# S5 readout from turned-back states, remainders of every third gate chunk by an adding DMA, and a Tanh behind the Sines

## The chip, the cores and the metric

The kernel runs on one core of one Trainium2 chip. The metric is the device time of one execution in microseconds; the time before is the median of three runs. PE is TensorE (PEld its weight load), DVE is VectorE, ACT is ScalarE, POOL is GpSimd, SP is SyncE. Two of these, SP and POOL, issue the kernel's DMAs.

## What is computed

Two layers of an encoder block on x of 256 frames by 1024 channels, in float32:

```
x += 1/2 * SwiGLU_FFN1(rmsnorm(x))
h = rmsnorm(x)
[u_s5 | q | k | v | z_conv | gate_logits] = h @ w_in
y_s5   = glu(gelu(S5(u_s5))) @ w_br_s5
y_attn = chunked_attention(q, k, v) @ w_br_attn
y_conv = conv_module(z_conv)            (ends in @ w_br_conv)
x += (sum over branches of sigmoid(gate_logits_i + b_i) * y_i) @ w_out
x += 1/2 * SwiGLU_FFN2(rmsnorm(x))
```

The S5 part is a complex diagonal recurrence over time, state[t] = a * state[t-1] + b u[t], in 16 groups of 64 states, and its output is the real part of c times the state plus d u.

## The kernel before

**Weights.** All weights are cut into 128x128 tiles, in the order in which PE reads them (`plan`), and eight tiles make a chunk of 128x1024 (512 KB). There are 382 chunks. For each chunk `fetch` (L391 to L407) loads `raw` on SP's queue (three slots), ACT rounds it to `hi` in the format fp32r (L403), and DVE subtracts to get the remainder `lo` (L404, L405); `hi` and `lo` have four slots each, so that the work on a chunk waits until PE has read the chunk four before it. PE makes each product from the pieces (`prod`, L419 to L439): `hi` with the rounded activations, `hi` with their remainder, and `lo` with the rounded activations. In the feed-forward parts the first two are one product of 512 columns; in the gates all three have 256 columns, and in q, k and v 512.

**Stages.** Per layer: up and down projection of FFN1, the mixer, FFN2. The mixer (L752) multiplies by w_in for the S5 input, the convolution's input (z), q, k and v, then by the 24 column blocks of the gates (23 in a row, one later), the branch projections and w_out. Attention, convolution and S5 run beside the gates' products.

**S5.** The recurrence is done in a rotating frame. `s5_tables` (L637) computes during FFN1's up projection tables of cosines and sines by frame, eight blocks j of 128 states, in `tab` (tile name `tbl`): `angle` prepares them, `sines` (L709) applies the Sine on ACT in two instructions of 128x2048, and `coefs` builds the readout matrices `cc`. In the mixer `s5_states(j)` (L775) copies the input rows to `us` (ACT copies for the first four blocks, 12 DMAs on POOL's queue for the last four), multiplies them by `bs` on PE into the one buffer `pq`, rotates the result with `sa` and `sc` on DVE, scans it over time, and multiplies the scanned values by cosines (into `mc`) and by sines (into `tab`). Every four blocks a readout on PE follows: for each of four column groups four products into `y`, with real part, negated imaginary part, negated real part and negated imaginary part of `cc`, two from `mc` and two from `tab`:

```
for n, (w, i) in enumerate(((0, 0), (2, 1), (1, 1), (2, 0))):
    for q in range(4):
        jj = 4 * b + q
        rhs = (mcs[jj][:, i * T:(i + 1) * T] if n < 2 else st["tab"][:, jj, i, :])
```

ACT's functions come from tables that an instruction ACT_TABLE_LOAD brings in: Sine is in one, Tanh and the exponential in another, and plain copies are in each. The compiler puts a load ahead of an instruction whose function is not in the table at hand.

**Order.** Every instruction is first recorded with the tiles that it reads and writes (`Recorder`), then a planner (`schedule`, L251, and `one_pass`, L288) puts them into one order per engine, by costs (`price`, L222) and due times counted back from PE's queue. The engines then run these orders, each waiting where data is not there. So a change of a cost or an instruction shifts the order elsewhere too. All instructions are issued from one line, L339 (L341 in the change), so that line tells nothing in the profile; the tiles do.

Of the kernel before, what the change touches and what calls it, by code (L numbers as in the profile page):

```python
# [17 lines left out]
F32 = mybir.dt.float32  # L18
F32R = mybir.dt.float32r
I32 = mybir.dt.int32  # L20
AF = mybir.ActivationFunctionType
ALU = mybir.AluOpType
# [3 lines left out]
L, P, T, DM, DFF = 2, 128, 256, 1024, 2816  # L26
# [4 lines left out]
U0, Q0, K0, V0, Z0, G0 = 0, 2, 6, 10, 14, 18  # L31
CHT = 8
# [48 lines left out]
PLAN = plan()  # L81
INDEX = {t: i for i, t in enumerate(PLAN)}
NCH = -(-len(PLAN) // CHT)


PCOLS = {}
# [41 lines left out]
class Recorder:  # L128
# [92 lines left out]
    @staticmethod  # L221
    def price(eng, name, outs, ins, kw):  # L222
        n = 1
        for d in list(outs[0].ap)[1:]:
            n *= d[1]
        if name == "dma_start":
            return (max(0.45, 1.5e-3 * n), 1.8) if eng == "sp" else (1.0, 2.0 + 2.5e-3 * n)
        if eng == "pe":
            if name == "transpose":
                return 0.1, 0.2  # L230
            if n == 1:
                return 0.224, 0.2
            if kw["rhs"].dtype != F32R or n < 256:
                rows = outs[0].partition_size()
                return max(n / 2370.0 * 4 * rows / P, 0.03), 0.2
            return n / 2240.0 + 0.006, 0.2
        scal = 0.06 if any(a.free_size() == 1 for a in ins) and n > 1 else 0
        psum = any(a.space == PSUM for a in outs + ins)
        if eng == "act":
            return 0.12 + n / 1200.0 + scal + (0.1 if kw.get("accum_out") is not None else 0), 0.2  # L240
        if name == "reciprocal":
            return 0.06 + 8 * n / 960.0, 0.16
        if name == "tensor_reduce":
            n = 1
            for d in list(ins[0].ap)[1:]:
                n *= d[1]
        fast = name in ("tensor_scalar", "tensor_copy") and not psum
        rate = 1920.0 if fast else 480.0 if name == "tensor_tensor_scan" else 960.0
        return 0.068 + scal + n / rate + (0.06 if kw.get("accum_out") is not None else 0), 0.16
# [103 lines left out]
class Builder:  # L353
# [37 lines left out]
    def fetch(self, upto):  # L391
        nc = self.nc
        while self.fetched <= min(upto, NCH - 1):
            c = self.fetched
            n = min(CHT, len(PLAN) - c * CHT) * P
            raw = self.tile(self.chunk, [P, CHT * P], F32, "raw", RAW)
            hi = self.tile(self.chunk, [P, CHT * P], F32R, "hi", 4)
            lo = self.tile(self.chunk, [P, CHT * P], F32R, "lo", 4)
            for a, b in PARTS.get(c, [(0, n)]):
                if (c, a) in X_LOADS:  # L400
                    self.load_x(*X_LOADS[c, a])
                nc.sync.dma_start(out=raw[:, a:b], in_=self.w_d[c, :, a:b])
                nc.scalar.copy(out=hi[:, a:b], in_=raw[:, a:b])  # L403
                nc.vector.tensor_tensor(out=lo[:, a:b], in0=raw[:, a:b], in1=hi[:, a:b].bitcast(F32),  # L404
                                        op=ALU.subtract)  # L405
            self.chunks[c] = (hi, lo)
            self.chunks.pop(c - 12, None)  # L407
            self.fetched += 1
# [228 lines left out]
    def s5_tables(self, l):  # L637

        nc = self.nc
# [69 lines left out]
        def sines():  # L709
            for h in range(2):  # L710
                t = st["tab"][:, 4 * h:4 * h + 4, :, :].rearrange("p j r s -> p (j r s)")
                nc.scalar.activation(out=t, in_=t, func=AF.Sin, scale=6.283185)

        steps.append(sines)

        def coefs():
            lr, li, mag = st["lr"], self.par(l, "lim"), st["mag"]
            ar, ai, den, cr, ci, t = (self.small(8, s) for s in ("ar", "ai", "den", "cr", "ci", "ct"))
            tt(out=ar, in0=st["cos"][:, :, 1:2].rearrange("p j o -> p (j o)"), in1=mag, op=ALU.mult)
            ts(out=ar, in0=ar, scalar1=1.0, scalar2=None, op0=ALU.subtract)  # L720
            tt(out=ai, in0=st["sin"][:, :, 1:2].rearrange("p j o -> p (j o)"), in1=mag, op=ALU.mult)
            tt(out=den, in0=lr, in1=lr, op=ALU.mult)
            tt(out=t, in0=li, in1=li, op=ALU.mult)
            tt(out=den, in0=den, in1=t, op=ALU.add)
            nc.vector.reciprocal(out=den, in_=den)
            tt(out=cr, in0=ar, in1=lr, op=ALU.mult)
            tt(out=t, in0=ai, in1=li, op=ALU.mult)
            tt(out=cr, in0=cr, in1=t, op=ALU.add)
            tt(out=cr, in0=cr, in1=den, op=ALU.mult)
            tt(out=ci, in0=ai, in1=lr, op=ALU.mult)  # L730
            tt(out=t, in0=ar, in1=li, op=ALU.mult)
            tt(out=ci, in0=ci, in1=t, op=ALU.subtract)
            tt(out=ci, in0=ci, in1=den, op=ALU.mult)

            c4 = st["ct"].rearrange("p (j r c) -> p j r c", j=8, r=2)
            cc = self.tile(self.res, [P, 8, 3, 32], F32, "cc")
            t2 = self.tmp("sa", 2 * T)[:, :T].rearrange("p (j c) -> p j c", j=8)
            b = lambda v: v.unsqueeze(2).broadcast_to([P, 8, 32])
            tt(out=cc[:, :, 0, :], in0=c4[:, :, 0, :], in1=b(cr), op=ALU.mult)
            tt(out=t2, in0=c4[:, :, 1, :], in1=b(ci), op=ALU.mult)  # L740
            tt(out=cc[:, :, 0, :], in0=cc[:, :, 0, :], in1=t2, op=ALU.subtract)
            ts(out=cc[:, :, 1, :], in0=cc[:, :, 0, :], scalar1=-1.0, scalar2=None, op0=ALU.mult)
            tt(out=cc[:, :, 2, :], in0=c4[:, :, 0, :], in1=b(ci), op=ALU.mult)
            tt(out=t2, in0=c4[:, :, 1, :], in1=b(cr), op=ALU.mult)
            stt(out=cc[:, :, 2, :], in0=cc[:, :, 2, :], scalar=-1.0, in1=t2, op0=ALU.mult, op1=ALU.subtract)
            st["cc"] = cc

        steps.append(coefs)
# [3 lines left out]
    def mixer(self, l, after):  # L752
        nc = self.nc
# [21 lines left out]
        def s5_states(j):  # L775
# [30 lines left out]
            mc = self.tmp("mc", 2 * T)  # L806
            tt(out=v3(mc), in0=v3(z), in1=b3(cosj), op=ALU.mult)
            tt(out=tab, in0=v3(z), in1=b3(sinj), op=ALU.mult)
            mcs.append(mc)
            if j % 4 == 3:  # L810
                b = j // 4
                if b == 0:
                    y_ps[0] = self.bank("y")
                cc = st["cc"]
                nc.together()
                for n, (w, i) in enumerate(((0, 0), (2, 1), (1, 1), (2, 0))):
                    for q in range(4):
                        jj = 4 * b + q
                        rhs = (mcs[jj][:, i * T:(i + 1) * T] if n < 2 else st["tab"][:, jj, i, :])
                        nc.tensor.matmul(y_ps[0][32 * q:32 * q + 32, b * T:(b + 1) * T], lhsT=cc[:, jj, w, :], rhs=rhs,  # L820
                                         start=n == 0, stop=n == 3, tile_position=(0, 32 * q))
                nc.apart()

        mcs = []
# [393 lines left out]
```

## Time and profile before

| | |
|---|---|
| runs | 1139.96 us median of 3 (1139.72 to 1142.24) |
| profiled execution, its own time | 1140.64 us |
| its span | 1138.8 us |
| PE busy | 1130.4 us (99%) |
| DVE busy | 993.3 us (87%) |
| ACT busy | 707.1 us (62%) |
| POOL busy | 13.0 us (1%) |
| share of the 16 DMA engines' time that SP's queue took | 56.3% |

The span is the time from the first to the last instruction. An engine's busy time is the union of its instructions' durations; matmuls overlap, so that their durations are longer than their distance. Idle time of an engine is put down to what ended it ("<-"). The chain of waits goes back from the last instruction, at each step to what released it.

### The profile page before, as it was taken

What the parts mean: (1) busy time and instruction counts of PE and PEld (TensorE: products, weight loads), DVE (VectorE), ACT (ScalarE), POOL (GpSimd) and SP (SyncE); (2) the same over time, 40 slices, a digit from 0 to 9 for tenths busy, and PEclk for the clock granted to TensorE, in tenths of its full rate; (3) what the DMA queues carried; (4) which work ended last, traced back from release to release, by engine and by line L of the source; (5) the groups of instructions that cost most, each with busy time, mean ns of one, the idle gap of its engine ahead of it and who ended that gap; (6) DMA issues with size and microseconds to landing.
All of it is one profiled execution on the core that took longest, in us unless ns stands there. A gap on an engine that the chain in (4) does not pass through costs nothing.

```text
span 1138.8 us, 19885 instructions
## 1 busy us (share of the span) xinstructions
PE 1130.4 (99%) x7246; PEld 1006.7 (88%) x7246; DVE 993.3 (87%) x2089; ACT 707.1 (62%) x1366; POOL 13.0 (1%) x32
## 2 busy tenths in 40 slices
PE   9999999999999999999999999999999999999998
PEld 6888888889999988888888888898899999888887
DVE  7999987999989988886789998879999898888754
ACT  6665765797674665555556657557877556655542
POOL 0000000010000000000000000002000000000000
PEclk9999999999999999999999999999999999999999
DMA  8655567555444665555565555666543556555662
GB/s 258 210 185 186 185 198 236 186 173 168 147 149 157 194 200 186 189 186 186 186 220 185 186 186 171 216 222 189 168 159 130 167 160 199 196 186 185 186 203 93
DMA packets 60322, 209.85 MB, mean 184 GB/s; under 512 B 6976, under 2 KB 9664, under 8 KB 59968
## 3 DMA queue, kind: packets, MB, share of 16 engines
q1 hardware_dynamic: 59072, 207.79, 56.3%
q8 instruction: 57, 0.93, 0.3%
q0 software_dynamic: 1152, 0.79, 0.3%
q14 instruction: 41, 0.34, 0.1%
HBM read 206.72 MB, written 1.05 MB: 182 GB/s over the span
## 4 chain that ended last, share of the span: by engine, by line
PE 96%; ACT 2%; issue 1%; DVE 1%; DMA 0%; SPq 0%; ACTq 0%; DVEq 0%
PE mm L339 65%; PE at L339 17%; PE y L339 7%; PE pq L339 6%; PE ax L339 1%; ACT hi L339 1%; ACT us L339 0%; DMA px<-in_x 0%; SPq L339 0%; DVE sa L339 0%; ACT L339 0%; DVE sc L339 0%; DVE lo L339 0%; ACT gh L339 0%; ACT x L339 0%
## 5 line engine op out<-in xcount | busy, mean ns | idle before, releaser
L339 ACT CAST hi<-raw 128x1024 fp32r<-128x1024 f32 (+1 forms) x385 | 400.5, 1042 | 291.5 <-PE mm L339 121.5
L339 DVE TENSOR_TENSOR lo<-raw,hi 128x1024 fp32r<-128x1024 f32 (+1 forms) x385 | 466.2, 1213 | 111.2 <-ACT hi L339 109.2
L339 PE MATMUL mm<-x,hi 128*128 128x256 f32 (+1 forms) x1600 | 406.3, 331 | 1.3 <-ACT hi L339 1.3
L339 PE MATMUL mm<-x,lo 128*128 128x256 f32 x1120 | 302.8, 282 | 0.1
L339 PEld LDWEIGHTS mm<-x,hi 128*128 128x128 f32 x1600 | 267.8, 188 | 26.5 <-ACT hi L339 2.7
L339 PE MATMUL mm<-AB,hi 128*128 128x512 f32 (+1 forms) x726 | 246.2, 390 | 0.0
L339 PEld LDWEIGHTS mm<-x,lo 128*128 128x128 f32 x1120 | 210.4, 188 | 9.8 <-issue 1.8
L339 PE MATMUL mm<-AB,lo 128*128 128x256 f32 x704 | 193.2, 281 | 0.0
L339 PEld LDWEIGHTS mm<-AB,hi 128*128 128x128 f32 x726 | 133.3, 188 | 28.4
L339 PEld LDWEIGHTS mm<-AB,lo 128*128 128x128 f32 x704 | 133.0, 189 | 2.6
L339 PE MATMUL at<-x,hi 128*128 128x512 f32 x384 | 135.3, 394 | 0.0
L339 PE MATMUL at<-x,lo 128*128 128x256 f32 x384 | 99.8, 279 | 0.0
L339 PEld LDWEIGHTS at<-x,hi 128*128 128x128 f32 x384 | 70.4, 187 | 13.1 <-issue 0.2
L339 PEld LDWEIGHTS at<-x,lo 128*128 128x128 f32 x384 | 72.0, 188 | 4.3
L339 PE MATMUL pq<-x,hi 128*128 128x512 f32 x192 | 69.4, 394 | 0.0
L339 PE MATMUL y<-x,hi 128*128 128x512 f32 x192 | 69.4, 394 | 0.0
L339 ACT CAST AB<-ev 128x256 fp32r<-128x256 f32 x88 | 35.8, 407 | 25.7 <-DVE ev L339 25.5
L339 DVE TENSOR_TENSOR ev<-mm,ev 128x256 f32<-128x256 f32 x111 | 45.5, 417 | 5.6 <-ACT ev L339 5.6
L339 PE MATMUL pq<-x,lo 128*128 128x256 f32 x192 | 49.8, 279 | 0.0
L339 PE MATMUL y<-x,lo 128*128 128x256 f32 x192 | 49.8, 279 | 0.0
L339 ACT COPY ev<-mm 128x256 f32<-128x256 f32 x111 | 39.9, 367 | 14.3 <-PE mm L339 13.0
L339 ACT ACTIVATE th<-ev 128x256 f32<-128x256 f32 x88 | 36.4, 418 | 19.0 <-DVE ev L339 18.7
(264 smaller groups left out, 1598.6 us busy)
## 6 DMA issues: line engine op xcount, KB each, us to landing
raw<-in_w SPq DMA_DIRECT2D x380, 512.0 KB, 4.2
AB<-in_b SPq DMA_DIRECT2D x2, 1536.0 KB, 7.5
mc<-in_s SPq DMA_DIRECT2D x8, 192.0 KB, 5.4
out_x<-px SPq DMA_DIRECT2D x8, 128.0 KB, 3.3
raw<-in_w SPq DMA_DIRECT2D x3, 256.0 KB, 4.6
px<-in_x SPq DMA_DIRECT2D x2, 256.0 KB, 6.0
ct<-in_p SPq DMA_DIRECT2D x2, 256.0 KB, 6.0
us<-gh POOLq DMA_DIRECT2D x16, 32.0 KB, 3.1
```

What stands on the lines that cost most here:

```text
L339: fn(*args, **kw)
```

## The change

Four edits. `s5_states` adds a subtraction and an addition of 128x256 on DVE per block that turn the scanned states back out of the rotating frame, into `mc`; the readout then takes two products per column group, both from `mc`, and `cc` loses the negated real part. For the chunks in `BY_DMA`, every third one that begins in the gates' columns (8 per layer), DVE's subtraction goes: ACT writes minus the rounded weights into `lo`, and a DMA on POOL's queue adds the weights to it, read from HBM again. A Tanh of one column follows the two Sines. The planner's cost of POOL's DMAs becomes 0.6 us and 7.0 us to the landing, whatever the size.

```diff
--- before.py
+++ after.py
@@ -81,6 +81,8 @@
 PLAN = plan()
 INDEX = {t: i for i, t in enumerate(PLAN)}
 NCH = -(-len(PLAN) // CHT)
+
+BY_DMA = [c for c in range(NCH) if PLAN[c * CHT][1] == "w_in" and PLAN[c * CHT][3] >= G0][::3]
 
 
 PCOLS = {}
@@ -224,7 +226,7 @@
         for d in list(outs[0].ap)[1:]:
             n *= d[1]
         if name == "dma_start":
-            return (max(0.45, 1.5e-3 * n), 1.8) if eng == "sp" else (1.0, 2.0 + 2.5e-3 * n)
+            return (max(0.45, 1.5e-3 * n), 1.8) if eng == "sp" else (0.6, 7.0)
         if eng == "pe":
             if name == "transpose":
                 return 0.1, 0.2
@@ -401,6 +403,11 @@
                     self.load_x(*X_LOADS[c, a])
                 nc.sync.dma_start(out=raw[:, a:b], in_=self.w_d[c, :, a:b])
                 nc.scalar.copy(out=hi[:, a:b], in_=raw[:, a:b])
+                if c in BY_DMA:
+
+                    nc.scalar.activation(out=lo, in_=raw, func=AF.Copy, scale=-1.0)
+                    nc.gpsimd.dma_start(out=lo, in_=self.w_d[c].bitcast(F32R), accum_op=ALU.add)
+                    continue
                 nc.vector.tensor_tensor(out=lo[:, a:b], in0=raw[:, a:b], in1=hi[:, a:b].bitcast(F32),
                                         op=ALU.subtract)
             self.chunks[c] = (hi, lo)
@@ -711,6 +718,8 @@
                 t = st["tab"][:, 4 * h:4 * h + 4, :, :].rearrange("p j r s -> p (j r s)")
                 nc.scalar.activation(out=t, in_=t, func=AF.Sin, scale=6.283185)
 
+            nc.scalar.activation(out=self.tanh, in_=st["sin"][:, 7, :1], func=AF.Tanh)
+
         steps.append(sines)
 
         def coefs():
@@ -733,16 +742,15 @@
             tt(out=ci, in0=ci, in1=den, op=ALU.mult)
 
             c4 = st["ct"].rearrange("p (j r c) -> p j r c", j=8, r=2)
-            cc = self.tile(self.res, [P, 8, 3, 32], F32, "cc")
+            cc = self.tile(self.res, [P, 8, 2, 32], F32, "cc")
             t2 = self.tmp("sa", 2 * T)[:, :T].rearrange("p (j c) -> p j c", j=8)
             b = lambda v: v.unsqueeze(2).broadcast_to([P, 8, 32])
             tt(out=cc[:, :, 0, :], in0=c4[:, :, 0, :], in1=b(cr), op=ALU.mult)
             tt(out=t2, in0=c4[:, :, 1, :], in1=b(ci), op=ALU.mult)
             tt(out=cc[:, :, 0, :], in0=cc[:, :, 0, :], in1=t2, op=ALU.subtract)
-            ts(out=cc[:, :, 1, :], in0=cc[:, :, 0, :], scalar1=-1.0, scalar2=None, op0=ALU.mult)
-            tt(out=cc[:, :, 2, :], in0=c4[:, :, 0, :], in1=b(ci), op=ALU.mult)
+            tt(out=cc[:, :, 1, :], in0=c4[:, :, 0, :], in1=b(ci), op=ALU.mult)
             tt(out=t2, in0=c4[:, :, 1, :], in1=b(cr), op=ALU.mult)
-            stt(out=cc[:, :, 2, :], in0=cc[:, :, 2, :], scalar=-1.0, in1=t2, op0=ALU.mult, op1=ALU.subtract)
+            stt(out=cc[:, :, 1, :], in0=cc[:, :, 1, :], scalar=-1.0, in1=t2, op0=ALU.mult, op1=ALU.subtract)
             st["cc"] = cc
 
         steps.append(coefs)
@@ -806,6 +814,8 @@
             mc = self.tmp("mc", 2 * T)
             tt(out=v3(mc), in0=v3(z), in1=b3(cosj), op=ALU.mult)
             tt(out=tab, in0=v3(z), in1=b3(sinj), op=ALU.mult)
+            tt(out=mc[:, :T], in0=mc[:, :T], in1=tab[:, 1, :], op=ALU.subtract)
+            tt(out=mc[:, T:], in0=mc[:, T:], in1=tab[:, 0, :], op=ALU.add)
             mcs.append(mc)
             if j % 4 == 3:
                 b = j // 4
@@ -813,12 +823,12 @@
                     y_ps[0] = self.bank("y")
                 cc = st["cc"]
                 nc.together()
-                for n, (w, i) in enumerate(((0, 0), (2, 1), (1, 1), (2, 0))):
+                for r in range(2):
                     for q in range(4):
                         jj = 4 * b + q
-                        rhs = (mcs[jj][:, i * T:(i + 1) * T] if n < 2 else st["tab"][:, jj, i, :])
-                        nc.tensor.matmul(y_ps[0][32 * q:32 * q + 32, b * T:(b + 1) * T], lhsT=cc[:, jj, w, :], rhs=rhs,
-                                         start=n == 0, stop=n == 3, tile_position=(0, 32 * q))
+                        nc.tensor.matmul(y_ps[0][32 * q:32 * q + 32, b * T:(b + 1) * T], lhsT=cc[:, jj, r, :],
+                                         rhs=mcs[jj][:, r * T:(r + 1) * T], start=r == 0, stop=r == 1,
+                                         tile_position=(0, 32 * q))
                 nc.apart()
 
         mcs = []
```

ACT's order at the first Tanh of the second layer's mixer (`th` of the convolution's gate, from `sc`; `us` the copies for S5, `hi` a rounded chunk). Before:

```order
L339 CAST us_1915<-gh_1723 32x256 x4
L339 CAST us_1915<-gl_1724 32x256
L339 CAST hi_1740<-raw_1739 128x1024
L339 ACT_TABLE_LOAD
L339 ACTIVATE th_1734<-sc_1733 128x256
L339 CAST us_1915<-gl_1724 32x256
```

In the change:

```order
L341 CAST us_1915<-gh_1723 32x256 x4
L341 CAST us_1915<-gl_1724 32x256 x2
L341 CAST hi_1740<-raw_1739 128x1024
L341 ACTIVATE th_1734<-sc_1733 128x256
L341 CAST us_1915<-gh_1723 32x256
```

The load of the table has left this place, and one copy into `us` has moved ahead of the cast.

DVE's order in the second layer's mixer up to the last reading of the second pair of S5 input products (`sc_1922`), which frees `pq` for the third pair. Before:

```order
L339 TENSOR_TENSOR lo_1750<-raw_1748,hi_1749 128x1024
L339 TENSOR_TENSOR sa_1921<-pq_1920,tbl_1325 128x512
L339 TENSOR_TENSOR sc_1742<-mm_1735,rb_1715 128x512
L339 TENSOR_TENSOR sa_1917<-sa_1917,sc_1918 128x256 x2
L339 TENSOR_TENSOR lo_1753<-raw_1751,hi_1752 128x1024
L339 SCALAR_TENSOR_TENSOR hp_1725<-th_1743,sc_1742 128x256
L339 SCALAR_TENSOR_TENSOR sa_1917<-mag_1374,sa_1917 128x256
L339 TENSOR_TENSOR sc_1922<-pq_1920,tbl_1325 128x512
```

In the change:

```order
L341 TENSOR_TENSOR lo_1750<-raw_1748,hi_1749 128x1024
L341 TENSOR_TENSOR sa_1921<-pq_1920,tbl_1325 128x512
L341 TENSOR_TENSOR sc_1742<-mm_1735,rb_1715 128x512
L341 TENSOR_TENSOR sa_1917<-sa_1917,sc_1918 128x256 x2
L341 SCALAR_TENSOR_TENSOR sa_1917<-mag_1374,sa_1917 128x256
L341 SCALAR_TENSOR_TENSOR hp_1725<-th_1743,sc_1742 128x256
L341 SCALAR_TENSOR_TENSOR sa_1917<-mag_1374,sa_1917 128x256
L341 TENSOR_TENSOR sc_1922<-pq_1920,tbl_1325 128x512
```

One remainder (`lo_1753`) now stands behind the reading, and the second scan (out of `mag`) ahead of it.

ACT's order at the first gate chunk of the second layer (`lo_1786` and `hi_1785`, from `raw_1784`; `jk` are sums of squares for the attention's norms). In the change:

```order
L341 ACTIVATE jk_1828,ss_1727_1824<-nat_1775 128x64
L341 ACTIVATE lo_1786<-raw_1784 128x1024
L341 CAST hi_1785<-raw_1784 128x1024
L341 CAST x_1520_1617<-ev_1791 128x256
```

and POOL's order around it:

```order
L341 DMA us_1933<-gl_1724 32x256
L341 DMA us_1933<-gh_1723 32x256
L341 DMA lo_1786<-in_w 128x1024
L341 DMA lo_1963<-in_w 128x1024
```

The negated rounded weights are written ahead of the cast, and the adding DMAs stand on POOL's queue behind the copies for S5. Before, `lo_1786` was a subtraction on DVE behind the cast.

## Rows read from the trace of the kernel before

**Rows 1.** The page, parts 1 and 2: PE's busy time; its granted clock in 40 slices.

```profile
PE 1130.4 (99%) x7246; PEld 1006.7 (88%) x7246; DVE 993.3 (87%) x2089; ACT 707.1 (62%) x1366; POOL 13.0 (1%) x32
...
PEclk9999999999999999999999999999999999999999
```

**Rows 2.** Waits of PE: us in total, times, longest us.

```profile
PE pq L339 <- DVE sc L339: 1.8, 2, 0.9
PE mm L339 <- ACT hi L339: 1.3, 2, 1.0
```

**Rows 3.** Both mixers: length, busy PE, PEld, DVE, ACT, POOL; clock, DMA share, GB/s.

```profile
198.00:390.00 192.00, 191.10 (x1485) 177.98 (x1484) 182.63 (x409) 134.62 (x316) 6.00 (x12) 1.00 0.53 171
763.00:950.00 187.00, 186.09 (x1453) 173.34 (x1451) 179.03 (x399) 133.94 (x315) 5.81 (x12) 1.00 0.52 167
```

**Rows 4.** Timeline of PE at the first readout: start us, us, instruction.

```profile
248.24 1.07 PE L339 MATMUL y<-mc,cc 128*32 128x256 f32 x16
249.13 1.05 PE L339 MATMUL y<-tbl,cc 128*32 128x256 f32 x16
250.11 0.50 PE L339 MATMUL at<-hi,x 128*128 128x512 f32 x1
```

**Rows 5.** Instructions on tile cc: count, shortest/median/longest ns, first and last start.

```profile
L339 PE MATMUL y<-tbl,cc x64: 379/379/379, 249.1 to 855.3; 128*32 128x256 f32 x64
...
L339 DVE TENSOR_SCALAR cc<-cc x2: 294/294/294, 159.3 to 713.1; 128x256 f32<-128x256 f32 x2
```

**Rows 6.** Groups by form, whole span: count, busy us, mean ns, idle before.

```profile
L339 DVE TENSOR_TENSOR lo<-raw,hi 128x1024 fp32r<-128x1024 f32 x380 | 463.3, 1221 | 109.9 <-ACT hi L339 108.1
L339 ACT CAST hi<-raw 128x1024 fp32r<-128x1024 f32 x380 | 397.8, 1049 | 290.5 <-PE mm L339 121.5 <-issue 65.3 <-PE at L339 42.4
...
L339 DVE TENSOR_TENSOR sa<-sa,sc 128x256 f32<-128x256 f32 x32 | 12.6, 414 | 0.0
```

**Rows 7.** Chain of waits at the second layer's third pair: start us, us, what.

```profile
771.52 1.28 ACT L339
...
781.10 0.68 DVE sc L339
...
781.92 0.47 PE pq L339 x2
782.39 2.79 PE at L339 x12
```

**Rows 8.** Timeline of DVE ahead of that pair, its idle time in brackets.

```profile
773.26 0.43 DVE L339 SCALAR_TENSOR_TENSOR hp<-th,sc 128x256 f32<-128x256 f32 x1 [0.50 <-ACT th L339]
...
776.02 1.23 DVE L339 TENSOR_TENSOR lo<-raw,hi 128x1024 fp32r<-128x1024 f32 x1 [1.14 <-ACT hi L339]
...
779.03 1.22 DVE L339 TENSOR_TENSOR lo<-raw,hi 128x1024 fp32r<-128x1024 f32 x1
780.17 0.42 DVE L339 SCALAR_TENSOR_TENSOR hp<-th,sc 128x256 f32<-128x256 f32 x1
```

**Rows 9.** Timeline of PE there, with products of 256 columns ahead of it.

```profile
772.17 0.28 PE L339 MATMUL mm<-x,lo 128*128 128x256 f32 x1
...
772.53 0.28 PE L339 MATMUL mm<-x,lo 128*128 128x256 f32 x1
...
780.61 0.40 PE L339 MATMUL at<-hi,x 128*128 128x512 f32 x1
781.92 0.36 PE L339 MATMUL pq<-us,bs 96*128 96x256 f32 x1 [0.91 <-DVE sc L339]
```

**Rows 10.** Tile us: POOL's issues of its copies (ns), and their landings.

```profile
L339 POOL DMA_DIRECT2D us<-gh x16: 492/497/632, 225.7 to 794.9; - x16
...
DMA to landing us min/median/max: 2.2/3.2/4.3
```

**Rows 11.** Tile raw, 198 to 350 us: landings of the loads of 512 KB.

```profile
DMA to landing us min/median/max: 3.5/3.7/4.8
```

**Rows 12.** Groups by form on DVE, 198 to 350 us: its longest TENSOR_SCALAR.

```profile
L339 DVE TENSOR_SCALAR cv<-hp,px,db 128x256 f32<-128x256 f32 x2 | 0.7, 408 | 0.0
```

## The prediction

> **What bounds the kernel now.** I read the engines' shares first. TensorE (PE) is busy 99% of the span at a granted clock of 9 tenths or more in every slice [rows 1]; so time can only go where its queue gets shorter or stops waiting. The list of waits of PE comes next: two waits of 0.9 us, where the S5 input products (`pq`) wait for VectorE (DVE), and two for ScalarE's casts (ACT), both at the start [rows 2]. The table by stretches shows the two mixers, 198 to 390 us and 763 to 950 us: PE has no room there, and DVE is busy 182.6 of 192 and 179.0 of 187 us, nearly as full; ScalarE (ACT) has some 53 us free in each [rows 3]. So in the mixers DVE is the engine that can hold PE up, and the change touches just that: it moves work among DVE, ACT and POOL's queue, and shortens PE's.
>
> **Readout by two products (PE).** Each layer has two readouts of four products per column group; the diff makes them two. In the trace the first readout starts at 248.24, its second half (the `tbl` operands, which go) at 249.13, the next product at 250.11 [rows 4]: a half is 0.89 to 0.98 us. There are four such halves, 64 records of `y` out of `tbl` [rows 5]. PE has no idle time around them, so this is a plain gain: 4 x 0.89 = **-3.6 us** (up to -3.9).
>
> **Turning the states back (DVE).** For it DVE gets 32 additions of 128x256, 0.41 us each [rows 6]: 16 x 0.41 = 6.6 us per layer. The negated copy of the coefficients goes (0.29 us) [rows 5]. Eight remainders of 128x1024 per layer leave DVE, 1.22 us each [rows 6]: 9.8 us. Net -3.5 us per mixer. On an engine beside PE that is worth nothing by itself; it pays for the longer S5 chain. Where it could still show is the first readout: behind the sixth pair of `pq` products the order of the change has on DVE three remainders, two scans, two full-width multiplies, the eight new additions, three other additions of that size and two small ones, about 9.8 us from start to start (1.14 a remainder [rows 8]), while PE has 40 products of 512 columns at 0.233 us (twelve in 2.79 [rows 7]) = 9.3 us plus the pair itself, 0.24 us. That is level. I take +0.1 us at this place and the one like it, +0.4 us in all; ends 0 and 2 us.
>
> **Tanh behind the Sines (ACT).** In the chain of waits the late `pq` goes back, through DVE and ACT, to a table load: the load of 1.28 us, then (left out in the rows) `th`, copies into `us`, a cast into `hi`, its remainder on DVE, `sa`, and last `sc` and PE [rows 7]. DVE idles 0.50 us before `hp` and 1.14 us before that remainder [rows 8]. The load sits in front of the mixer's first Tanh, because the last table function before it was a Sine. The change's dummy Tanh takes the load to the stretch behind the Sines, in the up projection, where PE has no wait [rows 2]; the number of loads stays. The order of the change has no load before `th` any more, so the casts behind it come 1.28 us sooner, less 0.41 us for one copy that moved ahead of it. In that order the third pair also waits for one remainder fewer on DVE (1.14 us from start to start [rows 8]) and one scan more. The wait of 0.91 us [rows 9] should go: 2 x 0.9 = **-1.8 us**. The ends are 0, and -2.1 us if the whole delay of 1.07 us goes each time (780.61 to 781.92, less the product's own 0.23 us [rows 9]).
>
> **Remainders by a DMA.** Per layer 8 of 24 gate chunks lose their subtraction on DVE. Instead ACT writes the negated rounded weights (16 passes of 128x1024; nearest row, the cast, 1.05 us [rows 6]: 8.4 us per mixer out of 53 us free [rows 3]), and a DMA on POOL's queue adds the weights to them from HBM. This read is 8 x 0.52 MB more per mixer, where the DMA engines are busy 52% [rows 3]. The subtraction's 1.2 us between cast and product becomes a DMA's landing, and PE's queue stops if it is late. How long it may take: a slot of `lo` is free when PE has read the chunk four before. The order of the change has 49 products between that and the first reading of the new remainder at the tightest place (37 of 512 columns, the halved readout, a `pq` pair), 8.7 + 0.9 + 0.5 = 9.8 us or so [rows 4, 7]; 74 to 81 of 256 columns (0.12 us each, three per 0.36 [rows 9]) with small ones between at the others, 10.1 to 11.7 us. Off go the pass on ACT (1.05 us) and some 0.35 us for two hand-overs and ACT's own queue. That leaves 8.4, 8.7 and 8.9 us for each layer's first three chunks and 9.5 to 10.3 us for the other five, from issue to landing.
>
> No row shows an accumulating DMA. The smallest thing on POOL's queue lands in 2.2 us (median 3.2, longest 4.3) and costs POOL 0.5 us [rows 10]; a plain load of the same size lands in 3.7 us in the mixer (longest 4.8) [rows 11]. Below, then, 2.2 us; above, POOL's longest and two whole loads, 4.3 + 2 x 4.8 = 13.9 us, as the adding reads slot and weights. I take the median of POOL's DMA and twice the part of a load that is not latency, 3.2 + 2 x (3.7 - 2.2) = 6.2 us, because the size and the traffic are those of the load row. That leaves over 2 us, so I cost this edit at **0**, and the cover is PE's own three chunks; when it is gone each late microsecond stops PE 16 times. POOL's queue holds nothing else there: its 12 small copies per layer stand ahead of the first added chunk, and a copy for the S5 inputs could delay it only if it were itself 8 us late. VectorE and SP wait for none of it; the next raw slot is now released by ACT.
>
> The Trainium skill, "DMA: Bandwidth & Descriptors", in "Anatomy of one DMA", gives for a plain DMA of this queue 2.0 us plus bytes over 436 GB/s, an estimate of 3.2 us here; it prices no adding. By that the sum would be the same.
>
> **The rest.** The planner's cost for POOL's DMAs rises for the copies as well, so the S5 copies and pairs come a little earlier in PE's order; no instruction comes with it. Two tiny Tanhs cost ACT 0.2 us each.
>
> **Sum**, on the profiled execution's 1140.64 us (span 1138.8 and 1.8 around it): -3.6 - 1.8 + 0.4 + 0 = -5.0, 1135.6 us. The median of the runs shown is 1139.96, 0.7 us less, so the forecast is **1135.0 us**.
>
> **Rivals.**
> 1. *The added chunk lands too late* (slower). For it: PE hangs on it 16 times with one slot's worth of lead, and its price is unknown. Against: even two plain loads one after the other would land in 7.4 us. Beyond 8.4 us the first chunks stop PE. At 9.4 us the loss is 1.0 + 0.7 + 0.5 = 2.2 us per layer, 4.4 in all: most of the gain. At 10 us it is 5.5 us per layer: 1135.0 + 11 = 1146 us. At 12 us, 21 per layer: 1177 us. It decides from about 9.7 us.
> 2. *The waits on DVE come back elsewhere.* The pairs stand closer in the new order (third and fourth 14 products apart, 3.3 us of PE against about 3.5 us of DVE work), and the readout is level. If two to four such places cost 0.5 to 0.9 us, only the readout's gain is left, less a little: 1137 to 1139, say 1138.4 us.
> 3. *POOL issues late.* POOL's 24 issues took 0.49 to 0.63 us beside a DVE that was 95% busy [rows 3, 10], so a busy DVE as such does not hold them. The Trainium skill, "SBUF — State Buffer", section "Who interferes with whom", says that descriptor making stops while a `tensor_scalar` or copy on VectorE holds the port that both share. By the trace this is at most one such instruction per DMA, 0.41 us for the longest in that stretch [rows 12]; it would need a landing already near 8.4 us, and then gives up to 16 x 0.4 = 6.4 us: 1141.4 us.
>
> That the change does not do what it says I leave out: the order shows the load moved, the products halved and 16 adding DMAs.
>
> **Chances.** Forecast 0.64; rival 1 0.17; rival 2 0.16; rival 3 0.03. A difference under 0.2% (2.3 us) cannot be told from none. Faster by more: the forecast and the lightest of rival 2, 0.65; within: most of rivals 2 and 3 and the light end of rival 1, 0.20; slower: the rest of rival 1, 0.15. The range begins where readout and wait give their most and nothing new waits, -6.0, with half a microsecond for the runs' scatter: 1133.4. It ends at 1142.5, a landing of about 9.8 us: above lies rival 1's tail, 0.15, below some 0.04. The forecast's own range is 1133.4 to 1137.
>
> **What would show it.** PE's `y` records 64 instead of 128. No `pq` wait on `sc` in the list of waits, and no table load between `hi` and `th` near 208 and 771 us. Adding DMAs landing in 5 to 8 us. Wrong: a PE wait on a DMA into `lo`, up to 16 times, near 250 to 325 and 813 to 889 us, or landings over 8.4 us; or `pq` and `y` waiting for `sa`, `sc` or `mc` of DVE by more than 0.5 us a place.

## The result and the profile after

The changed kernel took **1148.26 us** (median of 4 runs, 1147.0 to 1148.76), the kernel before 1140.33 us (4 runs, 1139.72 to 1142.24): ratio **1.0063**, 95% interval 1.0051 to 1.0076. Forecast were 1135.0 us and a range of 1133.4 to 1142.5. The change is slower by some 8 us, on the side that got a chance of 0.15. The profiled execution took 1148.76 us, its span 1147.0 against 1138.8.

First the page of the changed kernel: busy PE, its granted clock in 40 slices, and the two kinds of transfers of weights with their median landing.

```profile
PE 1132.6 (99%) x7182; PEld 1009.1 (88%) x7182; DVE 986.1 (86%) x2103; ACT 718.6 (63%) x1384; POOL 27.0 (2%) x48
...
PEclk9999999998999999999999999999989999999999
...
raw<-in_w SPq DMA_DIRECT2D x380, 512.0 KB, 4.0
lo<-in_w POOLq DMA_DIRECT2D x16, 512.0 KB, 6.2
```

PE's busy time grew by 2.2 us although 64 of its products are gone [rows 1], and two slices, one in each mixer, have a lower clock. The adding DMAs land in 6.2 us, as forecast. The waits of PE (us in total, times, longest) say where the time went:

```profile
PE at L341 <- ACT nat L341: 7.7, 2, 4.2
...
PE mm L341 <- ACT hi L341: 1.1, 2, 0.8
```

The two waits of `pq` for `sc` [rows 2] are gone. No wait on a DMA into `lo` has come. In their place stand two of a kind that no part of the prediction spoke of: the transposes of the normalized keys (`at<-ident,nat`) wait 4.2 and 3.6 us for ScalarE's 16 scalings of the keys k (`nat<-nat,y`). The mixers against [rows 3] (length, busy PE, PEld, DVE, ACT, POOL, clock, DMA share, GB/s):

```profile
198.00:390.00 192.00, 187.84 (x1431) 176.04 (x1430) 176.10 (x411) 138.12 (x321) 12.96 (x20) 0.98 0.64 188
763.00:950.00 187.00, 183.43 (x1396) 171.75 (x1395) 171.35 (x400) 134.48 (x315) 12.84 (x20) 0.98 0.66 191
```

VectorE is busy 6.5 and 7.7 us less in the same windows, and no wait of PE in the mixers is put down to it: rival 2 of the prediction has no part. The DMA engines are busy 64 and 66% instead of 53 and 52%. The halved readout is there, on PE's timeline in the first layer:

```profile
246.01 1.07 PE L341 MATMUL y<-mc,cc 128*32 128x256 f32 x16
247.01 0.50 PE L341 MATMUL at<-lo,x 128*128 128x512 f32 x1
```

1.00 us from the readout to the next product, where it was 1.87 [rows 4]: 0.87 us won, four times.

**Where the new wait comes from.** The chain of waits at the first layer's stop, followed back (start us, us, what):

```profile
260.53 1.12 DVE lo L341
...
261.67 7.75 DMA raw<-in_w
...
269.80 0.93 ACT hi L341
...
270.75 0.47 ACT AB L341
271.22 0.48 ACT nat L341 x2
...
271.75 0.48 PE at L341
```

PE waits for the scalings; they stand on ScalarE's queue behind the cast of chunk 92 (`hi`); the cast waits for that chunk's load, which lands 7.75 us after its issue instead of 3.7 [rows 11]. ScalarE's timeline shows it standing still:

```profile
263.30 1.06 ACT L341 CAST hi<-raw 128x1024 fp32r<-128x1024 f32 x1 [0.17 <-DMA raw<-in_w]
269.80 1.04 ACT L341 CAST hi<-raw 128x1024 fp32r<-128x1024 f32 x1 [5.44 <-DMA raw<-in_w]
270.75 0.47 ACT L341 ACTIVATE AB<-mm,hb 128x256 f32<-128x256 f32 x1
271.12 1.05 ACT L341 ACTIVATE nat<-nat,y 128x64 f32<-128x64 f32 x4
```

And the load is late because three transfers of 512 KB were issued within 0.7 us: POOL's third adding DMA (chunk 90) at 261.55, the load of chunk 92 at 261.67, when VectorE's remainder of chunk 89 had freed its slot, and the load of chunk 93 at 262.21. Tile `raw` at 261 to 263 us has the two loads and their landings:

```profile
L341 SPq DMA_DIRECT2D raw<-in_w x2: 328/328/328, 261.7 to 262.2; - x2
...
DMA to landing us min/median/max: 7.8/8.1/8.5
```

Tile `lo` over both mixers has those of the adding DMAs, and the longest, 8.2 us, is the one of chunk 90:

```profile
DMA to landing us min/median/max: 5.3/6.2/8.2
```

**What the stop costs.** Stretches around both stops (columns as in the table of the mixers):

```profile
264.00:267.30 3.30, 3.30 (x29) 3.30 (x29) 2.45 (x7) 0.36 (x1) 0.00 (x0) 1.00 0.94 250
267.30:270.90 3.60, 0.29 (x3) 0.08 (x1) 0.02 (x1) 1.10 (x2) 0.00 (x0) 1.00 0.92 307
270.90:277.70 6.80, 5.95 (x28) 5.95 (x29) 6.80 (x12) 5.76 (x20) 0.86 (x1) 0.50 0.53 119
...
837.50:844.30 6.80, 5.81 (x27) 5.81 (x28) 6.68 (x12) 5.77 (x21) 0.86 (x1) 0.50 0.57 133
```

PE's timeline at the first stop, and the same products farther on, up to the products of queries and keys (`at<-AB`):

```profile
267.31 0.28 PE L341 MATMUL mm<-x,hi 128*128 128x256 f32 x1
271.75 0.48 PE L341 MATMUL at<-ident,nat 128*128 128x128 f32 x1 [4.16 <-ACT nat L341]
...
281.44 0.93 PE L341 MATMUL at<-AB 64*128 64x128 f32 x8
```

From the last start before the stop to the first behind it are 4.44 us in the first layer and 3.86 in the second, where 0.12 is usual [rows 9]: stops of 4.32 and 3.74 us, 8.1 us in all. After each the granted clock is 0.50 (1.2 instead of 2.4 GHz) for 6.8 us. What that adds is read off the way from the first k transpose to the first product of queries and keys, 271.75 to 281.44 here: 9.7 us. In experiment 5 below, with the same order on PE and no stop there, it is 266.69 to 273.63, 6.9 us; in the second layer it is 9.6 against 6.9. The clock thus costs 2.7 + 2.7 = 5.4 us. Sum: readout -3.5, waits for `sc` -2.0 (measured alone in run 7), stops +8.1, clock +5.4, together +8.0 of the 8.2 that the span grew.

### The profile page after: what moved, and what is told of

It reads as the page before. It is cut to its first block, busy times and chain, and to the rows that moved or that the text cites. A ratio compares the mean times of both kernels' runs of the same rounds, so it can differ in the third digit from the quotient of the medians.

```text
span 1147.0 us, 19806 instructions
## 1 busy us (share of the span) xinstructions
PE 1132.6 (99%) x7182; PEld 1009.1 (88%) x7182; DVE 986.1 (86%) x2103; ACT 718.6 (63%) x1384; POOL 27.0 (2%) x48
## 4 chain that ended last, share of the span: by engine, by line
PE 96%; DMA 2%; DVE 1%; ACT 1%; SPq 0%; issue 0%; ACTq 0%; DVEq 0%
PE mm L341 65%; PE at L341 18%; PE pq L341 6%; PE y L341 6%; DMA raw<-in_w 1%; PE ax L341 1%; DMA px<-in_x 0%; DVE lo L341 0%; SPq L341 0%; ACT hi L341 0%; DVE sa L341 0%; ACT nat L341 0%; ACT x L341 0%; ACT AB L341 0%; ACT sq L341 0%
## 5 line engine op out<-in xcount | busy, mean ns | idle before, releaser
L341 DVE TENSOR_TENSOR lo<-raw,hi 128x1024 fp32r<-128x1024 f32 (+1 forms) x369 | 446.9, 1213 | 124.4 <-ACT hi L341 120.1
```

What stands on the lines that cost most here:

```text
L341: fn(*args, **kw)
```

## The experiments

The theory (A): each layer's third adding DMA collides with two loads; the order of the change puts the cast of the late load ahead of the scalings on ScalarE's in-order queue; PE stops and the clock falls. The main rival (B): the new order does it alone, and the DMA is innocent.

**1. No adding DMA.** The planner lays out the rest anew.

```
-BY_DMA = [c for c in range(NCH) if ... ][::3]
+BY_DMA = []
```

> The change without its adding DMAs: the list BY_DMA is empty, so every remainder is again a subtraction on VectorE; the halved readout and the early Tanh stay. Theory A (the adding DMA of each layer's third such chunk makes the load beside it land late, ScalarE's cast of that load stands ahead of the scalings of k, so PE stops some 4 us in each layer and then runs at a granted clock of 0.50 for 6.8 us): the stops of 4.2 and 3.6 us before the k transposes and both stretches at 0.50 are gone, and the two gains are left, -3.6 and -2.1 us: 1134.5 us or so, ratio 0.995. Rival B (the new order alone bunches the loads, or PE's shorter queue brings out a wait that was there all along): the stops stay, 1142 us or more. Rival C (VectorE holds PE up elsewhere once it has its remainders back): a wait of PE on sc or mc of over 0.5 us, 1137 to 1139 us.

1146.41 us, ratio 1.0051 (1.0036 to 1.0066). All three guesses missed: the stop before the k transposes is gone, yet the kernel is slow (rival B's time without B's stops). The waits of PE:

```profile
PE mm L341 <- ACT ct L341: 3.7, 3, 1.7
PE mm L341 <- DVE tbl L341: 1.5, 2, 0.8
```

They lie at the products of the convolution's branch (`ct`, 347 and 912 us) and of w_out (`tbl`, 366 and 932 us), some 100 us behind the first readout: in the chain of waits a chunk's remainder on VectorE, then `cv`, `hp` and ScalarE's `ct` in turn come late there. VectorE is at 185 of 192 us in the first mixer. Whether that is the order's doing or VectorE's being too full this run can't tell, since its order is another everywhere; the next runs hold the order.

**2. Adding DMAs of 128 columns**, the order untouched.

```
 for fn, args, kw in op.call:
+    if "accum_op" in kw:
+        kw = dict(kw, out=kw["out"][:, :P], in_=kw["in_"][:, :P])
     fn(*args, **kw)
```

> The change with its order of instructions untouched, but each of the 16 adding DMAs moves 128 of its 1024 columns (the remainders of the other seven tiles of those chunks lack the weights, which this kernel leaves out). Theory A (the bytes of the adding DMA take the DMA engines from the loads beside it): loads beside it land in under 4.5 us, no stop before the k transposes, granted clock 1.00 in both mixers, 1134.5 us (1133.5 to 1136). Rival B (the bunched loads, ScalarE's order and VectorE's late remainder do it by themselves): loads of 7 us or more stay, 1146 us or more. Halfway (1138 to 1144): both have a part.

1141.82 us, ratio 1.0009 (0.9999 to 1.0019): halfway. The loss is nearly gone, but PE still waits for the scalings, 2.5 us at most. Waits and, below, the chain there:

```profile
PE at L346 <- ACT nat L346: 4.7, 2, 2.5
```

```profile
261.10 6.07 DMA raw<-in_w
...
267.56 0.90 ACT hi L346
```

Two loads 0.44 us apart take 6.1 and 6.9 us even with an eighth of the adding bytes beside them. In the kernel before, the nearest two there start 1.8 us apart, and the slowest lands in 4.4. So B holds in part: the new order bunches the loads and puts the cast in front, and that alone stops PE 2.2 and 2.5 us; the other seven eighths of the adding bytes lengthen each stop by 1.3 to 1.7 us.

**3. Only the third adding DMA of each layer small**, the other 14 whole (the same lines, with a count: `n % 8 == 2`).

> As the kernel with the small adding DMAs, but only the third of each layer's eight (chunks 90 and 281) is cut to 128 columns; the other 14 are whole (left out: the weights in the remainders of seven tiles of these two chunks). Theory A, that just these two collide with the loads whose casts stand ahead of the scalings of k: the stops and the stretches at 0.50 go, 1134.5 us (1133.5 to 1136.5). If all 16 cost something each: between 1137 and 1147 us. Rival B: 1146 us or more.

1140.36 us, ratio 0.9995 (0.9986 to 1.0005), 7.9 us below the change. Making all 16 small gave no more than making these two small: the other 14 DMAs cost nothing that shows. The wait for the scalings stays about as in the run before (3.9 us in both layers together, 4.7 there), which is why it isn't the 1134.5 expected. It varies: beside the same small DMA the two loads land in 4.8 and 5.6 us in the first layer, and PE stops 1.2 us; in the second they land in 6.5 and 7.1 us, and it stops 2.7. What makes this difference is not shown.

**4. Scalings first.** All DMAs whole; on ScalarE the cast of chunk 92 (283 in the second layer) and the negation of chunk 93 that stands among the scalings of k go behind them. VectorE's remainder of chunk 92 follows its cast; nothing moves on PE, SP and POOL.

```
-for op in self.schedule():
+for op in self.moved(self.schedule()):
...
+    held = {op.seq for op in act[nats[0] - 2:nats[-1]] if tag(op) in (("hi", "raw"), ("lo", "raw"))}
+    # held operations are put out behind the last scaling
```

> The change whole, with one edit: on ScalarE the cast of chunk 92 (of 283 or so in the second layer, the same place) and the negation that stands among the scalings of k go behind those 16 scalings. The DMAs and loads stay as late as they are. Theory A (the late load costs because ScalarE's in-order queue has its cast ahead of the scalings): loads of 7 to 8.5 us stay, the stop before the k transposes and the stretch at 0.50 go, 1134.5 to 1136.5 us. Rival D (the late load is waited for somewhere anyway, by PE at the chunk's first product or by VectorE's remainder): the stop moves to the products of that chunk, 1138 us or more. Rival C (ScalarE's added passes make the scalings late by themselves): the stop stays, 1145 us or more.

1139.95 us (1137.4 to 1142.6), ratio 0.9993 (0.9984 to 1.0002): 8.3 us below the change, by the position of two of ScalarE's instructions in each layer, and of the remainder behind one of them. The profiled execution is the fastest of the ten (1137.4 us, span 1135.6); what the median has on top of it has no trace. In it the loads and the DMA of chunk 90 are later than ever, but ScalarE scales at 265.15, and the stop and the low clock are gone. What waits now is rival 1 of the prediction. Waits of PE, then tile `lo` at 260 to 262 us (chunk 90):

```profile
PE mm L341 <- DMA lo<-in_w: 1.7, 3, 0.9
```

```profile
L341 POOL DMA_DIRECT2D lo<-in_w x1: 856/856/856, 260.2 to 260.2; - x1
...
DMA to landing us min/median/max: 8.6/8.6/8.6
```

PE has waited 0.9 us for this one, so 7.7 us were available, where the prediction has 8.9 for the third chunk. Theory A's mechanism stands, its number was 4 us too low: the late transfers are waited for once more, farther down (rival D in part).

**5. Both: scalings first and the third DMA small.**

> The change with the scalings of k put first on ScalarE and the third adding DMA of each layer cut to 128 columns (left out: the weights in the remainders of seven tiles of chunks 90 and 281). Both suspected costs are gone, the order is else that of the change. Theory A: no wait of PE above 0.4 us between 200 and 950 us, granted clock 1.00, and both gains as forecast: 1140.7 less 5.5, 1135 us (1134.3 to 1136.3), ratio 0.995. If the forecast's gains themselves were too large, or a cost is spread over many places: 1137 us or more with no wait to show for it.

1138.53 us, ratio 0.9982 (0.9973 to 0.9991). With both suspected costs gone the loss is gone too, but only 2.2 of the expected 5.5 us are won. The profiled execution (span 1136.8) has one wait on a DMA of 1.1 us (chunk 93, whose negation now goes out beside the next load; it lands in 8.5 us) and none else in the mixers:

```profile
PE mm L346 <- DMA lo<-in_w: 1.1, 1, 1.1
```

The other 2.5 us or so are spread: added up from start to start over both mixers, the products of queries and keys (`at<-AB`) take 0.9 us more than before, the four readouts together 0.4 more than four times 1.00, and the products of 256 columns 1.2 more. This is the run that gives the time of the products behind the scalings without a stop; PE's timeline there:

```profile
266.69 0.27 PE L346 MATMUL at<-ident,nat 128*128 128x128 f32 x1
...
273.63 1.38 PE L346 MATMUL at<-AB 64*128 64x128 f32 x8
```

**6. Scalings first, and chunks 90 and 281 back on VectorE**, with 14 adding DMAs, and nothing left out.

```
+if c in BY_DMA[2::8]:
+    cast, neg, add = nc.ops[-3:]
+    neg.call, add.call = [], []
+    cast.call.append((nc.vector._real.tensor_tensor, (), dict(out=lo, in0=raw, in1=hi.bitcast(F32), op=ALU.subtract)))
```

> The change with the scalings of k put first and the remainder of chunks 90 and 281 subtracted on VectorE again (behind ScalarE's cast of the chunk), so that 14 adding DMAs are left; nothing of the computation is left out. The load that reused the raw slot comes 1.2 us later, which also pulls the two bunched loads apart. Theory A: the waits of 0.4 to 0.9 us for the DMAs that the kernel with the scalings first still has near 267 and 830 us are gone; VectorE is late by 1.2 us there, 0 to 0.6 us of it seen by PE: 1135.5 to 1137.5 us, below both kernels. Rival: VectorE has no room at that place and pq or the products of a chunk wait for it, 1138.5 to 1141 us.

1139.97 us, ratio 0.9995 (0.9986 to 1.0004). The rival came in: VectorE's 1.2 us at that place make the factor of the scalings (`y`) late (waits for `nat` of 0.7 us in each layer), and the DMA of chunk 93 still stops PE 0.9 and 0.4 us.

**7. The three edits one by one in the old order.** The planner plans the old program; only the instructions of an edit are exchanged at their place when it is written out. Nothing else moves, in this run and the next four. First the Tanh:

```
     nc.scalar.activation(out=t, in_=t, func=AF.Sin, scale=6.283185)
+nc.scalar.activation(out=self.tanh, in_=st["sin"][:, 7, :1], func=AF.Tanh)
```

> The kernel before with the early Tanh alone; every other instruction stands where it stood. The prediction's term for it: 1.8 to 2.1 us faster than before (ratio 0.9982 to 0.9984), the two waits of PE for sc gone. Rival: the wait goes to the next late thing in the chain and little is gained (ratio over 0.9995).

**1138.53 us, ratio 0.9982 (0.9972 to 0.9991)**, 2.0 us below before: the term as forecast. The list of waits has no `pq` on `sc`; two smaller ones are there instead, one of them at the first pair:

```profile
PE at L339 <- DVE ev L339: 0.8, 1, 0.8
PE pq L339 <- ACT us L339: 0.6, 1, 0.6
```

The profiled execution is the slowest of the ten (1139.69 us): in it the two new waits take back half of the gain. The one at the first pair (209 us) is of the kind that this run's rival speaks of; the other lies at 40 us, ahead of anything the edit touches. The median has the 2.0.

**8. The readout alone.** The additions are put right behind the multiply, the products halved in place.

```
+nc.ops[-1].group = nc.ops[-2].group = [2, [(vec.tensor_tensor, ...subtract), (vec.tensor_tensor, ...add)]]
...
+nc.ops[-1].call = [(matmul, ..., dict(lhsT=cc[:, jj, 2 * r, :], rhs=mcs[jj][:, r * T:(r + 1) * T], ...))]
```

> The kernel before with the halved readout alone, its two additions per step put right behind the multiply on VectorE, every other instruction held where it stood (so the planner finds no new order). The prediction's term: 3.6 to 3.9 us faster, ratio 0.9966 to 0.9968, with the two waits for sc still there. Rival: VectorE, 97% busy in the mixers and now given 6.6 us more in each without losing the remainders, makes pq, y or the products of a chunk wait: 0 to 3 us of the gain left, or a loss where PE's clock falls after a stop.

1152.0 us, ratio 1.01 (1.0085 to 1.0115): 11.5 us slower, worse than the rival. PE's waits, all new but the third:

```profile
PE at L339 <- ACT s L339: 2.8, 4, 0.8
PE pq L339 <- issue: 2.0, 4, 0.5
PE pq L339 <- DVE sc L339: 1.8, 2, 0.9
PE y L339 <- DVE mc L345: 1.4, 4, 0.4
PE at L339 <- ACT nat L339: 1.4, 2, 0.7
PE pq L339 <- DVE sa L339: 1.3, 2, 0.6
```

The readout itself, on PE's timeline:

```profile
249.56 0.63 PE L339 MATMUL y<-mc,cc 128*32 128x256 f32 x6
250.57 1.05 PE L339 MATMUL y<-mc,cc 128*32 128x256 f32 x10 [0.38 <-DVE mc L345]
251.55 0.50 PE L339 MATMUL at<-hi,x 128*128 128x512 f32 x1
```

It is no shorter in this run: 1.99 us to the next product, 1.87 before [rows 4], because its last products wait for the additions of the last block. So nothing is won on PE, and other chains through VectorE come 0.4 to 0.8 us late, again and again. Added up from start to start against before, 5.0 us go ahead of the `pq` pairs, 3.7 ahead of the transposes of the attention's weights (`s`), 1.7 ahead of those of `nat`, and 0.4 in the four readouts. VectorE has 8 or 9 us of idle time in each mixer, scattered, and gets 6.6 us more; whether it is too full or the additions stand in the wrong place of a held order, this run doesn't tell; run 11 says more.

**9. Readout and Tanh.**

> The two edits of the two kernels before this one together, order held as before, no adding DMA and VectorE with all its remainders. If both terms of the prediction hold without the DMAs: 5.4 to 6 us faster, 1135 us, ratio 0.9950. If VectorE is too full for it: waits of PE on sc, mc or lo, and a ratio between 0.997 and 1.002.

1149.25 us, ratio 1.0077 (1.0062 to 1.0092), 2.75 us below the readout alone. The two waits for `sc` are gone, the others stay. It is outside both guesses: the additions cost more than I allowed.

**10. The adding DMAs alone.**

```
+if c in BY_DMA:
+    nc.ops[-1].call = [(scalar.activation, ..., scale=-1.0), (gpsimd.dma_start, ..., accum_op=ALU.add)]
```

> The kernel before with the adding DMAs alone: in the place of VectorE's subtraction of those 16 chunks stand ScalarE's negation and the DMA, every other instruction held where it stood. From the start of the subtraction to PE's first reading of the remainder the trace of before has 8.7, 6.7, 8.8, 9.0, 11.5, 10.5, 9.0 and 8.6 us in the first layer; less 1.4 us for negation and hand-over that leaves 7.2, 5.3, 7.4, 7.6, 10.1, 9.1, 7.6 and 7.2. If the adding DMA lands in 5.4 us alone and 7 to 8 beside loads, the second chunk (87) stops PE 0.1 to 2 us in each layer, one or two more a little, and the time is 0 to 5 us above before. If the cost came with the planner's new order alone: no stop before the k transposes, the same time as before or up to 2 us less (the waits for sc are shorter with less on VectorE). If the adding DMA delays loads and casts as such, whatever the order: a stop before the k transposes here too, and 5 us or more above before.

1152.92 us, ratio 1.0113 (1.0084 to 1.0141), more than expected.

```profile
PE mm L341 <- DMA lo<-in_w: 7.8, 7, 1.9
PE pq L341 <- DVE sc L341: 1.8, 2, 0.9
```

```profile
DMA to landing us min/median/max: 7.1/8.0/8.8
```

No stop before the transposes: with the scalings ahead of the cast, that cost doesn't arise. But an adding DMA issued where the subtraction stood is late by up to 1.9 us for PE (behind the stop of that length the granted clock is 0.64 in the first layer, from 264 to 267 us, and 0.61 in the second, from 834 to 838), and never lands in under 7.1 us, since the next load goes out 0.3 us before it each time (issue at 243.06 and 243.34 us, 255.28 and 255.56, and so on): ScalarE's negation is the last reader of the slot as well as the writer for the DMA.

**11. All three in the old order.**

> All three edits (halved readout, early Tanh, adding DMAs) in the old order of instructions: only what an edit itself adds or removes differs from before. Held alone, the readout cost 11.5 us and the DMAs 12.4 us, the Tanh gave 2.0. If those are independent: 1140.5 + 11.5 + 12.4 - 2.0 = 1162 us or so. If the readout's loss came from VectorE being too full, which the DMAs relieve: its waits on sa, nat, s and mc shrink, those on the DMAs into lo stay (7.8 us of stops and a lower clock behind them), 1146 to 1152 us; then the two edits need each other, and what is left is the DMAs' landing alone.

1155.15 us, ratio 1.0129 (1.0116 to 1.0143). Between the two guesses (1162 and 1146 to 1152), so the relief is partial: waits for `sa`, `s` and `nat` fall from 5.5 (run 8) to 3.2 us, that of `y` on `mc` goes, those on the DMAs rise to 9.3 us. The four readouts, 1.9 to 2.0 us to the next product in run 8, take 1.2 to 1.3 here: in the same order, with the remainders gone, the additions come nearly in time. (PE's stops on the DMAs give VectorE time as well, so this is not all due to the remainders.)

**12. The DMA without its adding**, order untouched.

```
-nc.gpsimd.dma_start(out=lo, in_=self.w_d[c].bitcast(F32R), accum_op=ALU.add)
+nc.gpsimd.dma_start(out=lo, in_=self.w_d[c].bitcast(F32R))
```

> The change with its order untouched, the 16 DMAs on POOL's queue copying the weights plainly (left out: the addition; the remainder holds the unrounded weights). It tells whether it is the adding or the bytes that make the DMA long and its neighbours slow. If the adding (reading the slot and the weights): landing 3.5 to 4 us alone instead of 5.4, about 6 us beside two loads, those loads under 7 us, the stop before the k transposes 2.5 to 3.5 us, 1140 to 1146 us. If a POOL transfer of this size is as slow without adding: landings 5.4 to 8 us and 1147 to 1149 us as before.

1146.3 us (2 runs, 1144.86 to 1147.75), ratio 1.005 (1.0032 to 1.0069): at the edge of the first guess, with stops of 6.7 us in all (7.7 in the change). Tile `lo` at the second DMA, beside which no load is issued within a microsecond, and then the same in the changed kernel:

```profile
L341 POOL DMA_DIRECT2D lo<-in_w x1: 532/532/532, 249.7 to 249.7; - x1
...
DMA to landing us min/median/max: 3.7/3.7/3.7
```

```profile
L341 POOL DMA_DIRECT2D lo<-in_w x1: 870/870/870, 250.6 to 250.6; - x1
...
DMA to landing us min/median/max: 5.3/5.3/5.3
```

Alone, adding costs 1.6 us of landing. In the bunch it matters less: 7.3 us for the copy at 260.68, 7.0 and 7.8 for the two loads beside it, 0.7 to 0.9 us under the change. It is mostly the third 512 KB that counts.

**The version that beats both** is the smallest, the Tanh alone: 1138.53 us, 0.9982 of before (0.9972 to 0.9991).

## Why the prediction was wrong

- **Readout: right on PE.** -3.6 (up to -3.9) was forecast, 4 x 0.87 = 3.5 us measured in the change. What it needs of VectorE was right there too: no wait of PE in the mixers is put down to VectorE (rival 2). Runs 1 and 8, with all remainders on VectorE, have such waits.
- **Tanh: right.** -1.8 to -2.1 forecast, -2.0 us by itself (run 7, by the median), and the two waits for `sc` went as foretold.
- **Landing of the adding DMA: right in its number, in part by luck.** 6.2 us forecast, 6.2 us in the median; no PE wait on it in the changed kernel. Alone it lands in 5.3 us; the slow ones lift the median, and those stand beside loads, a meeting for which the sum has no term. The time available was read too long: the prediction's 8.7 + 0.9 + 0.5 is 10.1, not 9.8 (which comes out with the pair's 0.24 us that it gives elsewhere), and run 4 shows 7.7 us for the third chunk, where it has 8.9. So a landing of 8.2 to 8.6 us stops PE 0.4 to 1.1 us as soon as nothing else does (runs 4 to 6). Rival 1 was real, hidden behind a larger cost.
- **POOL's issues (rival 3): no part.** An issue took 0.86 us, no PE wait goes back to one.
- **The step that failed** is "so I cost this edit at **0**, and the cover is PE's own three chunks". I asked only who reads what the DMA writes. Two other things were in it. It takes the DMA engines from loads issued beside it (7.75 and 8.5 us instead of 3.7), and those loads feed ScalarE. And ScalarE's queue is in order: "VectorE and SP wait for none of it" left out what stands behind a cast there. I read ScalarE as 53 us free and did not list what is queued behind a late cast; the order of the change has the 16 scalings of k behind it, with one instruction between, and behind them PE. Runs 3 and 4 show it from both ends: with the third DMA small, or with the scalings ahead of the cast, the 8 us are gone.
- **A second step not taken.** I compared the new order at the places where the diff acts, the S5 pairs and the readout. Where it hurt is a place that no edit touches: the remainder of chunk 89, the loads of chunks 92 and 93 and the scalings of k had changed places in the planner's new order. Whether its new prices or the new instructions moved them, no run separates. Run 2 shows this part nearly alone: stops of 2.2 and 2.5 us.
- **The clock** was not in the sum. A stop of 3.7 to 4.3 us was followed by 6.8 us at a granted clock of 0.50, 2.7 us a layer on top. Behind shorter stops it differed: in run 2 the clock fell after 2.5 us and not after 2.2, in run 3 after 2.7 us and not after 1.2, in run 10 after 1.9 us in both layers.
- **The gain itself** would not have been -5.0: with both costs gone 2.2 us are left (run 5). My +0.4 for small new waits was some 3 us too low, in pieces of at most 1.1 us.

That the edits depend on each other and on their order is shown by runs 8 to 11: the readout loses 11.5 us where VectorE keeps its remainders, the DMAs lose 12.4 us where the order isn't laid out for them, and together in that order they lose less than the sum. Not settled is which of the small pieces in run 5 belong to the order and which to the loads.

## What to carry to other kernels

A transfer that is added to a busy stretch can be charged to its neighbours first: list what is issued within a microsecond of it, who reads those transfers, and what is queued behind that reader on its in-order engine, however idle the engine looks. Where a planner sets the order, a change moves work that the diff never names; go through the whole stretch for instructions that changed places around a load's reader, and above all put short work that PE waits for ahead of a cast that may be late. Exchanging an edit's instructions in a held order, one edit at a time, helps to tell a term from the order it came with; but a held order brings costs of its own (run 8), so read PE's timeline at the edit before the total.

## What was not expected of the hardware

- An adding DMA of 512 KB on POOL's queue landed in 5.3 us with little beside it, 8.2 to 8.6 us beside two loads; the plain copy in 3.7 and 7.3. The Trainium skill, "DMA: Bandwidth & Descriptors", section "Anatomy of one DMA", gives by an estimate 3.2 us for the plain one; the trace has 0.5 us more, and the adding is another 1.6.
- Issuing it took POOL 0.86 us, the plain copy 0.53.
- Two loads of 512 KB 0.4 us apart, with a small adding DMA, took 6.1 and 6.9 us in run 2 and 4.8 and 5.6 in run 3, though the DMA engines were busy only 56 to 65% of the mixer: a mean share says nothing of a bunch. In the first layer's bunch of the changed kernel the share was 0.92 to 0.94, at 250 to 307 GB/s.
- Stops of 4.3 and 3.7 us cost 2.7 us more each by the clock behind them.
